# A log-sum-exp scan over rows: 512-row tiles, 32 KiB descriptors, results over the inputs, and the running total by an fp32 broadcast matmul

## The chip, the cores and the metric

The kernel runs on one core of one Trainium2 chip. In the profile of the kernel before, PE multiplies matrices (1,945 matmul records), with the sums in the memory called PSUM; ACT (ScalarE, 385 instructions) and DVE (VectorE, 128) work element by element; SP (SyncE) issues the 128 loads and ACT the 128 stores; 16 DMA engines move the data, in packets. A packet is one record of the trace; here each contiguous run of 16 KiB is one (32,768 records). A packet of 4 bytes is called a semaphore packet: the trace has 16 of them for each load and each store (4,096 in all). The metric is the device time of one execution in microseconds (us). A version is compared with the kernel before it by runs of both on the same chip in the same rounds. A ratio is the mean time of one kernel's runs over the mean of the other's runs of the same rounds, so it is not quite the ratio of the medians that are quoted.

## The reference

```python
B, S, D = 8, 4096, 2048            # x is float32
out[:, 0, :] = x[:, 0, :]
for t in range(1, S):              # out[t] = log(exp(out[t-1]) + exp(x[t]))
    mx = np.maximum(out[:, t-1, :], x[:, t, :])
    out[:, t, :] = mx + np.log(np.exp(out[:, t-1, :] - mx) + np.exp(x[:, t, :] - mx))
```

This is log(cumsum(exp(x))) along the rows of each batch. 268.44 MB are read and 268.44 MB written, by any kernel.

## The kernel before

A tile is 256 rows of one batch: partition p holds rows 2p and 2p+1, which lie next to each other in memory, so each partition's run is 16 KiB. ACT takes exp of the tile into bf16. PE sums over the partitions with triangular matrices: `Li` (inclusive) for the first row, `Ls` (exclusive) for the second, into a PSUM tile of 2,048 columns. The first row's result is the log of PSUM; the second row adds its own exp on VectorE (DVE) first. The complementary triangles `Ui` and `Us` then complete the PSUM tile to the running total, which stays in PSUM for the next tile. Two batches alternate.

```python
xt = xpool.tile([P, 2 * D], f32);  nc.sync.dma_start(out=xt, in_=x_v[b, k])      # 4 buffers
et = epool.tile([P, 2 * D], bf16); nc.scalar.activation(et, xt, ACT.Exp)
for c in range(NC):                                     # 4 chunks of 512 columns
    nc.tensor.matmul(ps[:, lo:hi], Li, et[:, lo:hi], ...)
    nc.tensor.matmul(ps[:, lo:hi], Ls, et[:, D+lo:D+hi], ...)
ot = opool.tile([P, 2 * D], f32)                                                 # 4 buffers
nc.scalar.activation(ot[:, :D], ps, ACT.Ln)
nc.vector.tensor_add(ot[:, D:], ps, et[:, D:])
nc.scalar.activation(ot[:, D:], ot[:, D:], ACT.Ln)
nc.scalar.dma_start(out=o_v[b, k], in_=ot)
# ... then, for all but the last tile, matmuls with Ui and Us into the same ps
```

The softmax here doesn't subtract the row's maximum and nothing guards it: scores larger than these inputs give would overflow.

Of the kernel before, what the change touches and what calls it, by code (L numbers as in the profile page):

```python
# [1 line left out]

# [4 lines left out]


@with_exitstack
def kernel(  # L10
    ctx: ExitStack,
    tc: tile.TileContext,
    x: bass.AP,
    out: bass.AP,
):
    nc = tc.nc
    nc.scalar.preload_act_table_set("natural_log_exp_and_others")  # L17
    f32 = mybir.dt.float32
    bf16 = mybir.dt.bfloat16
    ACT = mybir.ActivationFunctionType  # L20

    B, S, D = x.shape
    P = 128
    SB = 256
    NBLK = S // SB
    FD = 512
    NC = D // FD
    PAIR = 2

    const = ctx.enter_context(tc.tile_pool(name="const", bufs=1))  # L30
    Li = const.tile([P, P], bf16)
    masks.make_upper_triangular(nc, Li, val=1.0, diag=True)
    Ls = const.tile([P, P], bf16)
    masks.make_upper_triangular(nc, Ls, val=1.0, diag=False)
    Ui = const.tile([P, P], bf16)
    masks.make_lower_triangular(nc, Ui, val=1.0, diag=False)
    Us = const.tile([P, P], bf16)
    masks.make_lower_triangular(nc, Us, val=1.0, diag=True)

    xpool = ctx.enter_context(tc.tile_pool(name="xpool", bufs=4))  # L40
    epool = ctx.enter_context(tc.tile_pool(name="epool", bufs=4))
    opool = ctx.enter_context(tc.tile_pool(name="opool", bufs=4))
    ppool = ctx.enter_context(tc.tile_pool(name="ppool", bufs=1, space=bass.MemoryType.PSUM))

    x_v = x.rearrange("b (k p two) d -> b k p (two d)", p=P, two=2)
    o_v = out.rearrange("b (k p two) d -> b k p (two d)", p=P, two=2)

    for bp in range(0, B, PAIR):
        psums = [
            ppool.tile([P, D], f32, name=f"ps_{bp}_{j}", tag=f"ps{j}")  # L50
            for j in range(PAIR)
        ]
        for k in range(NBLK):
            for j in range(PAIR):
                b = bp + j
                ps = psums[j]

                xt = xpool.tile([P, 2 * D], f32)
                nc.sync.dma_start(out=xt, in_=x_v[b, k])  # L59

                et = epool.tile([P, 2 * D], bf16)
                nc.scalar.activation(et, xt, ACT.Exp)  # L62

                for c in range(NC):
                    lo, hi = c * FD, (c + 1) * FD
                    nc.tensor.matmul(  # L66
                        ps[:, lo:hi], Li, et[:, lo:hi],
                        start=(k == 0), stop=False, skip_group_check=True,
                    )
                    nc.tensor.matmul(  # L70
                        ps[:, lo:hi], Ls, et[:, D + lo : D + hi],
                        start=False, stop=False, skip_group_check=True,
                    )

                ot = opool.tile([P, 2 * D], f32)
                nc.scalar.activation(ot[:, :D], ps, ACT.Ln)  # L76
                nc.vector.tensor_add(ot[:, D:], ps, et[:, D:])  # L77
                nc.scalar.activation(ot[:, D:], ot[:, D:], ACT.Ln)  # L78

                nc.scalar.dma_start(out=o_v[b, k], in_=ot)  # L80

                if k < NBLK - 1:
                    for c in range(NC):
                        lo, hi = c * FD, (c + 1) * FD
                        nc.tensor.matmul(  # L85
                            ps[:, lo:hi], Ui, et[:, lo:hi],
                            start=False, stop=False, skip_group_check=True,
                        )
                        nc.tensor.matmul(  # L89
                            ps[:, lo:hi], Us, et[:, D + lo : D + hi],  # L90
                            start=False, stop=False, skip_group_check=True,
                        )


# [1 line left out]
_INS = ['x']  # L96
_OUTS = [((8, 4096, 2048), 'float32')]


# [23 lines left out]
```

## Time and profile before

| | before |
|---|---|
| time, median of 3 | 1259.54 us (1259.22 to 1260.03) |
| span of the profiled execution | 1257.6 us |
| 16 KiB data packets | 32,768 |
| rate in the middle of the run | 430.5 GB/s (packet records, 120 to 1100 us) |

These are lines of the page of the kernel before: the span, the engines' busy time, the busy share of the DMA engines and their rate in 40 slices of the span, the packets, the DMA queues (q1 carries the loads, q10 the stores, q8 and q14 are named "instruction" by the trace), and the chain of waits by engine and by line.

```profile
span 1257.6 us, 5168 instructions
...
PE 645.3 (51%) x1945; PEld 239.4 (19%) x1984; DVE 293.0 (23%) x128; ACT 915.9 (73%) x385; POOL 1.9 (0%) x12
...
DMA  9999999999999999999999999999999999999997
GB/s 390 429 431 432 431 430 430 431 431 430 431 430 433 430 430 432 430 431 430 431 431 431 429 433 430 430 431 430 433 429 431 430 429 433 431 431 430 433 430 326
DMA packets 36888, 537.21 MB, mean 427 GB/s; under 512 B 4096, under 2 KB 4096, under 8 KB 4096
...
q1 hardware_dynamic: 18432, 268.44, 50.0%
q10 hardware_dynamic: 18432, 268.44, 49.9%
q8 instruction: 15, 0.25, 0.1%
q14 instruction: 9, 0.07, 0.0%
...
DMA 71%; ACT 26%; PE 1%; issue 1%; DVE 0%; ACTq 0%; SPq 0%
```

The DMA row is full in every slice but the last, and no compute engine is above 73%.

These are groups of the same page: line, engine, operation, shapes, count, then busy time and the mean of one in ns, then the idle time before them and what ended it.

```profile
L77 DVE TENSOR_TENSOR ot<-ps,et 128x2048 f32<-128x2048 f32 x128 | 293.0, 2291 | 949.4 <-ACT ot L76 949.4
L76 ACT ACTIVATE ot<-ps 128x2048 f32<-128x2048 f32 x128 | 239.8, 1873 | 319.2 <-DMA out_dram<-ot 284.9
L62 ACT ACTIVATE et<-xt 128x4096 bf16<-128x4096 f32 x128 | 461.7, 3607 | 7.9 <-DMA xt<-in_x_dram 7.9
```

ACT waits 285 us for stores to free an output buffer and only 8 us for loads: a DMA-bound kernel whose stores hold everything up.

These are stages of the same execution (from and to in us, length, busy time of each engine with counts, PE clock, share of the 16 DMA engines in use, GB/s): one in the middle and three at the end.

```profile
120.00:600.00 480.00, 255.20 (x753) 93.90 (x768) 112.29 (x49) 347.59 (x147) 0.00 (x0) 0.73 1.01 431
...
1232.00:1238.00 6.00, 5.41 (x20) 1.92 (x17) 0.05 (x1) 5.92 (x3) 0.00 (x0) 0.80 1.02 434
1238.00:1244.00 6.00, 0.09 (x1) 0.00 (x0) 4.43 (x2) 5.19 (x3) 0.00 (x0) 0.76 0.54 229
1244.00:1251.00 7.00, 0.00 (x0) 0.00 (x0) 0.00 (x0) 0.51 (x1) 0.00 (x0) 0.50 0.98 414
```

The DMA share falls to 0.54 from 1238 to 1244 us, while ACT and DVE finish the last two tiles.

### The profile page before, as it was taken

The numbers are of one execution on the slowest core, as the hardware profiler recorded it, in microseconds if no ns is written. First come the engines' busy times: TensorE is split into PE (matmuls) and PEld (weight loads), VectorE is DVE, ScalarE is ACT, GpSimd is POOL, SyncE is SP. The second block draws the span as 40 slices with busy tenths as digits, with TensorE's granted clock in tenths as the row PEclk, the third lists the DMA queues.
The fourth block names the chain that finished last, engine by engine and source line by source line (L and its number), as shares of the span: only waits on it lengthen the run. The fifth ranks groups of instructions, "written<-read, shape, count | busy, mean of one in ns | idle before, by whom it ended". The sixth has DMA issues, their size and how long they took to land.

```text
span 1257.6 us, 5168 instructions
## 1 busy us (share of the span) xinstructions
PE 645.3 (51%) x1945; PEld 239.4 (19%) x1984; DVE 293.0 (23%) x128; ACT 915.9 (73%) x385; POOL 1.9 (0%) x12
## 2 busy tenths in 40 slices
PE   3554554554545555455354555455544454555542
PEld 1221211121112222122111221112211121112210
DVE  1222222222222222222222222222222222222222
ACT  7976667777777777766777777777776666777775
POOL 0000000000000000000000000000000000000000
PEclk9877767776777687776668677786778878677686
DMA  9999999999999999999999999999999999999997
GB/s 390 429 431 432 431 430 430 431 431 430 431 430 433 430 430 432 430 431 430 431 431 431 429 433 430 430 431 430 433 429 431 430 429 433 431 431 430 433 430 326
DMA packets 36888, 537.21 MB, mean 427 GB/s; under 512 B 4096, under 2 KB 4096, under 8 KB 4096
## 3 DMA queue, kind: packets, MB, share of 16 engines
q1 hardware_dynamic: 18432, 268.44, 50.0%
q10 hardware_dynamic: 18432, 268.44, 49.9%
q8 instruction: 15, 0.25, 0.1%
q14 instruction: 9, 0.07, 0.0%
HBM read 268.44 MB, written 268.44 MB: 427 GB/s over the span
## 4 chain that ended last, share of the span: by engine, by line
DMA 71%; ACT 26%; PE 1%; issue 1%; DVE 0%; ACTq 0%; SPq 0%
DMA out_dram<-ot 70%; ACT et L62 13%; ACT ot L76 7%; ACT ot L78 7%; DMA xt<-in_x_dram 1%; DVE ot L77 0%; PE ps L66 0%; PE ps L70 0%; PE ps L85 0%; PE ps L89 0%; ACTq L76 0%; ACTq L80 0%; SPq L59 0%
## 5 line engine op out<-in xcount | busy, mean ns | idle before, releaser
L85 PE MATMUL ps<-et,Ui 128*128 128x512 bf16 x480 | 265.4, 553 | 511.6 <-DVE ot L77 509.2
L77 DVE TENSOR_TENSOR ot<-ps,et 128x2048 f32<-128x2048 f32 x128 | 293.0, 2291 | 949.4 <-ACT ot L76 949.4
L76 ACT ACTIVATE ot<-ps 128x2048 f32<-128x2048 f32 x128 | 239.8, 1873 | 319.2 <-DMA out_dram<-ot 284.9
L62 ACT ACTIVATE et<-xt 128x4096 bf16<-128x4096 f32 x128 | 461.7, 3607 | 7.9 <-DMA xt<-in_x_dram 7.9
L66 PE MATMUL ps<-et,Li 128*128 128x512 bf16 x512 | 228.0, 445 | 81.2 <-ACT et L62 79.6
L89 PE MATMUL ps<-et,Us 128*128 128x512 bf16 x463 | 261.9, 566 | 0.0
L78 ACT ACTIVATE ot<-ot 128x2048 f32<-128x2048 f32 x128 | 238.9, 1899 | 0.7 <-DVE ot L77 0.7
L70 PE MATMUL ps<-et,Ls 128*128 128x512 bf16 x490 | 211.0, 431 | 0.0
L89 PEld LDWEIGHTS <-Us 128*128 128x128 bf16 x480 | 61.1, 127 | 630.0 <-issue 618.7
L70 PEld LDWEIGHTS <-Ls 128*128 128x128 bf16 x512 | 57.7, 113 | 170.8 <-issue 137.0
L85 PEld LDWEIGHTS <-Ui 128*128 128x128 bf16 x480 | 61.0, 127 | 99.1 <-issue 74.5
L66 PEld LDWEIGHTS <-Li 128*128 128x128 bf16 x512 | 59.7, 117 | 98.1 <-issue 59.6
L17 ACT ACT_TABLE_LOAD x1 | 1.3, 1283 | 0.8 <-PEq L107 0.8
masks.py:102 POOL TENSOR_SCALAR_AFFINE_SELECT Us<-Us 128x128 bf16<-128x128 bf16 x1 | 0.3, 293 | 0.0
masks.py:66 POOL TENSOR_SCALAR_AFFINE_SELECT Li<-Li 128x128 bf16<-128x128 bf16 x1 | 0.3, 292 | 0.0
masks.py:66 POOL TENSOR_SCALAR_AFFINE_SELECT Ls<-Ls 128x128 bf16<-128x128 bf16 x1 | 0.3, 292 | 0.0
masks.py:102 POOL TENSOR_SCALAR_AFFINE_SELECT Ui<-Ui 128x128 bf16<-128x128 bf16 x1 | 0.3, 292 | 0.0
masks.py:65 POOL MEMSET Li<- 128x128 bf16 x1 | 0.2, 204 | 0.3 <-POOLq L107 0.3
masks.py:65 POOL MEMSET Ls<- 128x128 bf16 x1 | 0.2, 204 | 0.0
masks.py:101 POOL MEMSET Ui<- 128x128 bf16 x1 | 0.2, 204 | 0.0
masks.py:101 POOL MEMSET Us<- 128x128 bf16 x1 | 0.2, 204 | 0.0
L107 POOL MEMSET const-bfloat16-1.0<- 128x1 bf16 x1 | 0.1, 101 | 0.0
(3 smaller groups left out, 0.3 us busy)
## 6 DMA issues: line engine op xcount, KB each, us to landing
xt<-in_x_dram SPq DMA_DIRECT2D x128, 2048.0 KB, 28.7
out_dram<-ot ACTq DMA_DIRECT2D x128, 2048.0 KB, 30.0
```

What stands on the lines that cost most here:

```text
L17: nc.scalar.preload_act_table_set("natural_log_exp_and_others")
L62: nc.scalar.activation(et, xt, ACT.Exp)
L66: nc.tensor.matmul(ps[:, lo:hi], Li, et[:, lo:hi], start=(k == 0), stop=False, skip_group_check=True,)
L70: nc.tensor.matmul(ps[:, lo:hi], Ls, et[:, D + lo : D + hi], start=False, stop=False, skip_group_check=True,)
L76: nc.scalar.activation(ot[:, :D], ps, ACT.Ln)
L77: nc.vector.tensor_add(ot[:, D:], ps, et[:, D:])
L78: nc.scalar.activation(ot[:, D:], ot[:, D:], ACT.Ln)
L85: nc.tensor.matmul(ps[:, lo:hi], Ui, et[:, lo:hi], start=False, stop=False, skip_group_check=True,)
L89: nc.tensor.matmul(ps[:, lo:hi], Us, et[:, D + lo : D + hi], start=False, stop=False, skip_group_check=True,)
L107: nc = _bacc.Bacc("TRN2", target_bir_lowering=False, num_devices=1)
```

## The change

The intent is fewer and larger DMA packets, and a shorter tail. A tile becomes 512 rows (4 rows a partition, 32 KiB runs); the results overwrite the inputs in one pool of five 4 MB tiles; the work inside a tile goes in pieces of 512 columns; the last tile is also loaded and stored in those pieces, in 2 KiB descriptors. DVE copies the first row's sums out of PSUM and adds the other rows one after another. The total of a piece is the last partition's last row, spread to all partitions of the next tile's PSUM bank by an fp32 matmul with a matrix that is 1 in its last row; `Ui` and `Us` go. The core of the diff:

```diff
-    SB = 256
+    R = 4
+    LAG = 2
-    xpool = ctx.enter_context(tc.tile_pool(name="xpool", bufs=4))
-    opool = ctx.enter_context(tc.tile_pool(name="opool", bufs=4))
+    iopool = ctx.enter_context(tc.tile_pool(name="iopool", bufs=5))
+    spool = ctx.enter_context(tc.tile_pool(name="spool", bufs=3))
+    def load(b, k):
+        t = iopool.tile([P, R, D], f32, name=f"io_{b}_{k}", tag="io")
+        if (b, k) == tiles[-1]:
+            for c in range(NC):
+                nc.sync.dma_start(out=t[:, :, cols(c)], in_=x_v[b, k][:, :, cols(c)])
+        else:
+            nc.sync.dma_start(out=t, in_=x_v[b, k])
+    def front(b, k, c):                       # load at c == 0
+        nc.scalar.activation(et, t[:, :, cols(c)], ACT.Exp)
+        for r in range(R):
+            nc.tensor.matmul(ps, Li if r == 0 else Ls, et[:, r, :], ...)
+        nc.vector.tensor_copy(st[:, 0, :], ps)
+        for r in range(1, R):
+            nc.vector.tensor_add(st[:, r, :], st[:, r - 1, :], et[:, r, :])
+    def carry(b, k, c):
+        nc.tensor.matmul(bank(b, k + 1, c), last, sums[b, k, c][:, R - 1, :], start=True, ...)
+    def back(b, k, c):
+        nc.scalar.activation(t[:, :, cols(c)], sums.pop((b, k, c)), ACT.Ln)
+        if (b, k) == tiles[-1]:
+            nc.scalar.dma_start(out=o_v[b, k][:, :, cols(c)], in_=t[:, :, cols(c)])
+        elif c == NC - 1:
+            nc.scalar.dma_start(out=o_v[b, k], in_=t)
+    for n, piece in enumerate(pieces):
+        front(*piece)
+        if n >= 1:
+            carry(*pieces[n - 1])
+        if n >= LAG:
+            back(*pieces[n - LAG])
```

(`...` in it marks arguments that were cut; the removed loop is the one shown in the section before last.)

More of the change, by code (lines that the diff above doesn't have):

```diff
@@ L16 @@
     nc = tc.nc
-    nc.scalar.preload_act_table_set("natural_log_exp_and_others")
     f32 = mybir.dt.float32
@@ L20 @@
     ACT = mybir.ActivationFunctionType
+    nc.scalar.preload_act_table_set("natural_log_exp_and_others")
     B, S, D = x.shape
     P = 128
-    SB = 256
-    NBLK = S // SB
+    R = 4
+    NBLK = S // (P * R)
     FD = 512
     NC = D // FD
-    PAIR = 2
+    LAG = 2
     const = ctx.enter_context(tc.tile_pool(name="const", bufs=1))
@@ L34 @@
     masks.make_upper_triangular(nc, Ls, val=1.0, diag=False)
-    Ui = const.tile([P, P], bf16)
-    masks.make_lower_triangular(nc, Ui, val=1.0, diag=False)
-    Us = const.tile([P, P], bf16)
-    masks.make_lower_triangular(nc, Us, val=1.0, diag=True)
-    xpool = ctx.enter_context(tc.tile_pool(name="xpool", bufs=4))
-    epool = ctx.enter_context(tc.tile_pool(name="epool", bufs=4))
-    opool = ctx.enter_context(tc.tile_pool(name="opool", bufs=4))
-    ppool = ctx.enter_context(tc.tile_pool(name="ppool", bufs=1, space=bass.MemoryType.PSUM))
@@ L45 @@
-    x_v = x.rearrange("b (k p two) d -> b k p (two d)", p=P, two=2)
-    o_v = out.rearrange("b (k p two) d -> b k p (two d)", p=P, two=2)
-    for bp in range(0, B, PAIR):
-        psums = [
-            ppool.tile([P, D], f32, name=f"ps_{bp}_{j}", tag=f"ps{j}")
-            for j in range(PAIR)
-        ]
-        for k in range(NBLK):
-            for j in range(PAIR):
-                b = bp + j
-                ps = psums[j]
-                xt = xpool.tile([P, 2 * D], f32)
-                nc.sync.dma_start(out=xt, in_=x_v[b, k])
-                et = epool.tile([P, 2 * D], bf16)
-                nc.scalar.activation(et, xt, ACT.Exp)
-                for c in range(NC):
-                    lo, hi = c * FD, (c + 1) * FD
-                    nc.tensor.matmul(
-                        ps[:, lo:hi], Li, et[:, lo:hi],
-                        start=(k == 0), stop=False, skip_group_check=True,
-                    )
-                    nc.tensor.matmul(
-                        ps[:, lo:hi], Ls, et[:, D + lo : D + hi],
-                        start=False, stop=False, skip_group_check=True,
-                    )
-                ot = opool.tile([P, 2 * D], f32)
-                nc.scalar.activation(ot[:, :D], ps, ACT.Ln)
-                nc.vector.tensor_add(ot[:, D:], ps, et[:, D:])
-                nc.scalar.activation(ot[:, D:], ot[:, D:], ACT.Ln)
-                nc.scalar.dma_start(out=o_v[b, k], in_=ot)
-                if k < NBLK - 1:
-                    for c in range(NC):
-                        lo, hi = c * FD, (c + 1) * FD
-                        nc.tensor.matmul(
-                            ps[:, lo:hi], Ui, et[:, lo:hi],
-                            start=False, stop=False, skip_group_check=True,
-                        )
-                        nc.tensor.matmul(
-                            ps[:, lo:hi], Us, et[:, D + lo : D + hi],
-                            start=False, stop=False, skip_group_check=True,
-                        )
@@ new lines @@
+    last = const.tile([P, P], f32)
+    nc.gpsimd.memset(last, 1.0)
+    nc.gpsimd.affine_select(
+        out=last, in_=last, compare_op=mybir.AluOpType.is_ge, fill=0.0,
+        base=-(P - 1), pattern=[[0, P]], channel_multiplier=1,
+    )
+    iopool = ctx.enter_context(tc.tile_pool(name="iopool", bufs=5))
+    epool = ctx.enter_context(tc.tile_pool(name="epool", bufs=4))
+    spool = ctx.enter_context(tc.tile_pool(name="spool", bufs=3))
+    ppool = ctx.enter_context(tc.tile_pool(name="ppool", bufs=2, space=bass.MemoryType.PSUM))
@@ new lines, with cols @@
+    x_v = x.rearrange("b (k p r) d -> b k p r d", p=P, r=R)
+    o_v = out.rearrange("b (k p r) d -> b k p r d", p=P, r=R)
+    tiles = [(b, k) for b in range(B) for k in range(NBLK)]
+    pieces = [(b, k, c) for b, k in tiles for c in range(NC)]
+    io = {}
+    sums = {}
+    banks = {}
+    def cols(c):
+        return slice(c * FD, (c + 1) * FD)
+    def load(b, k):
+        t = iopool.tile([P, R, D], f32, name=f"io_{b}_{k}", tag="io")
+        io[b, k] = t
+        if (b, k) == tiles[-1]:
[3 more added lines that the diff above has]
+            nc.sync.dma_start(out=t, in_=x_v[b, k])
@@ new lines, in bank @@
+    def bank(b, k, c):
+        if (b, k, c) not in banks:
+            banks[b, k, c] = ppool.tile([P, FD], f32, name=f"ps_{b}_{k}_{c}", tag=f"ps{c}")
+        return banks[b, k, c]
+    def front(b, k, c):
+        if c == 0:
+            load(b, k)
+        t = io[b, k]
+        et = epool.tile([P, R, FD], bf16, name="et")
+        nc.scalar.activation(et, t[:, :, cols(c)], ACT.Exp)
+        ps = bank(b, k, c)
+        for r in range(R):
+            nc.tensor.matmul(
+                ps, Li if r == 0 else Ls, et[:, r, :],
+                start=(k == 0 and r == 0), stop=(r == R - 1), skip_group_check=True,
+            )
+        st = spool.tile([P, R, FD], f32, name="st")
+        nc.vector.tensor_copy(st[:, 0, :], ps)
+        for r in range(1, R):
+            nc.vector.tensor_add(st[:, r, :], st[:, r - 1, :], et[:, r, :])
+        sums[b, k, c] = st
@@ new lines, in carry @@
+    def carry(b, k, c):
+        if k < NBLK - 1:
+            nc.tensor.matmul(
+                bank(b, k + 1, c), last, sums[b, k, c][:, R - 1, :],
+                start=True, stop=False, skip_group_check=True,
+            )
+    def back(b, k, c):
+        t = io[b, k]
+        nc.scalar.activation(t[:, :, cols(c)], sums.pop((b, k, c)), ACT.Ln)
[3 more added lines that the diff above has]
+            nc.scalar.dma_start(out=o_v[b, k], in_=t)
@@ L96 @@
+    for n, piece in enumerate(pieces):
[4 more added lines that the diff above has]
+            back(*pieces[n - LAG])
+    for piece in pieces[-LAG:]:
+        back(*piece)
 _INS = ['x']
```

## The prediction

> **What bounds the kernel now.** The DMA engines: on the page DMA is 9 tenths in every slice but the last, and 429 to 433 GB/s move in nearly all; the stage table gives DMA share 1.01 at 431 GB/s from 60 to 1230 us. ACT is busy 73%, PE 51%, DVE 23%. In the chain of waits 70% is the store of results. 268.44 MB are read and as many written; the change leaves that so.
>
> In the packet records a 16 KiB packet takes 611 ns, an 8 KiB one (instruction load) 309 ns at best, a semaphore packet 9 ns. A line through the two sizes (estimate): 302 ns per 8 KiB plus 7 ns a packet. [...]
>
> **Terms on the critical path, per DMA engine:**
> - 2,048 packets of 16 KiB become 1,008 of 32 KiB plus the last tile's; 7 ns each: about -7 us.
> - Semaphore packets: 256 to about 134, at 9 ns: -1 us.
> - The last tile goes in 512-column chunks of 2 KiB descriptors: 256 packets at an estimated 82 ns against 16 of 1,215 ns: +1.7 us.
> - End: before, the packet records show the engines emptying between the last two stores (down to 1 of 16 in use), about 2.8 us lost, as ACT still works on the last pair of tiles. After, stores of two earlier 4 MB tiles (about 20 us) still queue while the last pieces are computed: -2.5 us.
> - Start: first packet 1.8 us into the span, as before; five loads (about 48 us) are queued until stores begin: 0.
>
> **Off the path:**
> - ACT: 512 exps and logs of 128x2048 at about 1.9 us (from 3,607 ns for 4,096 columns, 1,899 for 2,048): 970 us, 78%; per tile 15 us against 19.5 us of DMA.
> - DVE: 2,048 columns take 2.29 us, so 512 about 0.7 us; four a piece, 256 pieces: 710 us, 57%.
> - PE: per piece four bf16 matmuls of 430 to 560 ns and the carry. [...] The carry is needed four pieces later and the bank is doubled, so its latency hides.
> - The log of a tile's last two pieces now stands on ACT behind the next tile's exp, so the store waits for the next load; five buffers (97 us of period) cover a lifetime of about 20 load + 20 wait + 8 + 20 store.
>
> **Prediction.** Span 1257.6 - 7 - 1 + 1.7 - 2.5 = 1248.5; the time lies 1.9 us above the span: 1250 us, 0.8% faster, 8 in 10 between 1244 and 1258. Faster by over 2%: 1%. Within 2%: 94%. Slower by over 2%: 5%.
>
> **What would show it.** About 22,400 packets instead of 36,888, a 32 KiB packet at about 1,215 ns; 432 to 434 GB/s in the middle slices; a last slice well above 326 GB/s; DMA 9 tenths throughout; ACT waiting for loads, not for stores; PE waits not on the chain.
>
> **What would make it wrong.** 32 KiB descriptors are split (then about 1257), or the wider pitch slows HBM; [...] the store held behind the next load starves the load queue, showing as DMA gaps once a tile; 2 KiB packets cost far more than 82 ns.

1257.6 - 7 - 1 + 1.7 - 2.5 is 1248.8, where the prediction has 1248.5; with the 1.9 us on top that is 1250.7, where it has 1250. The 0.7 us for 512 columns on DVE is the estimate; a quarter of the 2.29 us would be 0.57.

## The result

| | before | after |
|---|---|---|
| time, median of 4 | 1259.38 us | 1259.70 us (1259.63 to 1259.88) |
| ratio to before | 1 | 1.0002 (0.9985 to 1.0019) |
| span | 1257.6 us | 1257.9 us |
| rate, 120 to 1100 us | 430.5 GB/s | 432.4 GB/s |
| a large data packet | 611 ns for 16 KiB | 1,213 ns for 32 KiB |

The change is worth nothing, where 9 us were forecast and 1244 us to 1258 us was the range. Lines of the page of the kernel after, as of before:

```profile
span 1257.9 us, 5492 instructions
...
PE 638.5 (51%) x1472; PEld 215.0 (17%) x1472; DVE 703.3 (56%) x1024; ACT 930.0 (74%) x513; POOL 1.5 (0%) x10
...
DMA  9999999999999999999999999999999999999997
GB/s 400 433 429 431 432 432 433 432 432 433 433 434 433 429 433 433 432 433 432 432 433 432 433 432 433 432 433 433 434 433 432 434 433 431 433 433 433 433 381 299
DMA packets 22399, 537.22 MB, mean 427 GB/s; under 512 B 2144, under 2 KB 2144, under 8 KB 6240
...
q1 hardware_dynamic: 11184, 268.44, 49.7%
q10 hardware_dynamic: 11184, 268.44, 49.6%
q8 instruction: 11, 0.18, 0.1%
q14 instruction: 20, 0.16, 0.0%
...
DMA 69%; ACT 14%; DVE 5%; PE 5%; issue 5%; SPq 1%; ACTq 0%; DVEq 0%
```

The packets did become 32 KiB (16,128 of them), the packet count of 22,399 is the predicted one, and the middle slices rose from about 431 to 433. What was won there was lost in the last two slices: 381 and 299 instead of 430 and 326. And q14 fetches 20 packets of instructions instead of 9, while DVE has 1,024 instructions instead of 128 (below, with 768 of them, q14 has 16).

The groups that answer to those of before:

```profile
L98 DVE TENSOR_TENSOR st<-st,et 128x512 f32<-128x512 f32 x768 | 530.9, 692 | 43.4
L110 ACT ACTIVATE io<-st 128x2048 f32<-128x2048 f32 x256 | 484.6, 1894 | 15.0 <-DMA io<-in_x_dram 10.7
L88 ACT ACTIVATE et<-io 128x2048 bf16<-128x2048 f32 x256 | 485.3, 1897 | 301.1 <-DMA io<-in_x_dram 301.1
L103 PE MATMUL ps<-st,last 128*128 128x512 f32 x448 | 304.6, 769 | 137.8 <-DVE st L98 136.6
```

ACT now waits for loads (311.8 us) and not for stores, as forecast, and the durations on ACT (1,897 and 1,894 ns) and DVE (692 ns) are near their estimates. The carry appears as two matmul records of 769 ns (448 records for 224 carries), 1.5 us in all.

The stages at the end of the kernel after:

```profile
120.00:600.00 480.00, 244.89 (x563) 83.43 (x564) 268.35 (x391) 354.64 (x197) 0.00 (x0) 0.77 1.00 432
...
1220.00:1226.00 6.00, 0.00 (x0) 0.00 (x0) 0.37 (x1) 0.00 (x0) 0.00 (x0) 0.57 0.58 216
1226.00:1232.00 6.00, 2.71 (x6) 1.21 (x6) 0.69 (x1) 4.67 (x3) 0.00 (x0) 0.50 0.48 171
1232.00:1238.00 6.00, 3.67 (x10) 0.93 (x8) 5.12 (x8) 6.00 (x4) 0.00 (x0) 0.78 0.52 220
```

For 18 us the DMA engines are half idle. ACT's own timeline there (start, length, what; in brackets the wait before it):

```profile
1214.67 1.90 ACT L110 ACTIVATE io<-st 128x2048 f32<-128x2048 f32 x1
1227.33 1.91 ACT L88 ACTIVATE et<-io 128x2048 bf16<-128x2048 f32 x1 [10.77 <-DMA io<-in_x_dram]
...
1234.67 0.34 ACTq L114 DMA_DIRECT2D out_dram<-io  x1
```

ACT waits 10.8 us for the first chunk of the last tile, and the store of the tile before it, which stands behind that on ACT, is issued only at 1234.7 us, when the store queue has been empty for about 9 us even on the DMA engine that is last.

The packet records (start, queue, size and duration of each packet; they do not name the DMA engine) show why that chunk was late. From 1199 to 1208 us both queues had work:

```
after, 1199 to 1208 us     mean engines in use    GB/s
load of the last tile       1.09 of 16            27     (2 KiB packets of 84 ns)
stores                     14.97 of 16            403    (32 KiB packets of 1,213 ns)
```

In these 9 us 112 load packets and 112 store packets began. If an engine takes one packet from each queue in turn, the load's share of time is 84 / (84 + 1213) = 6.5%, or 1.04 of 16 engines. The trace agrees with such turns, of one 2 KiB or one 32 KiB record. So in this stretch the small packets got little beside the large ones.

### The profile page after: what moved, and what is told of

It is laid out like the page before. It is cut to its first block, busy times and chain, and to the rows that moved or that the text cites. A ratio compares the mean times of both kernels' runs of the same rounds, so it can differ in the third digit from the quotient of the medians.

```text
span 1257.9 us, 5492 instructions
## 1 busy us (share of the span) xinstructions
PE 638.5 (51%) x1472; PEld 215.0 (17%) x1472; DVE 703.3 (56%) x1024; ACT 930.0 (74%) x513; POOL 1.5 (0%) x10
## 2 busy tenths in 40 slices
DMA packets 22399, 537.22 MB, mean 427 GB/s; under 512 B 2144, under 2 KB 2144, under 8 KB 6240
## 4 chain that ended last, share of the span: by engine, by line
DMA 69%; ACT 14%; DVE 5%; PE 5%; issue 5%; SPq 1%; ACTq 0%; DVEq 0%
DMA io<-in_x_dram 67%; ACT io L110 8%; ACT et L88 5%; DVE st L98 4%; PE ps L91 3%; DMA out_dram<-io 2%; PE ps L103 2%; DVE st L96 1%; SPq L74 1%; ACTq L114 0%; ACTq L110 0%; DVEq L98 0%; ACTq L88 0%; DVEq L96 0%; SPq L76 0%
## 5 line engine op out<-in xcount | busy, mean ns | idle before, releaser
L88 ACT ACTIVATE et<-io 128x2048 bf16<-128x2048 f32 x256 | 485.3, 1897 | 301.1 <-DMA io<-in_x_dram 301.1
L98 DVE TENSOR_TENSOR st<-st,et 128x512 f32<-128x512 f32 x768 | 530.9, 692 | 43.4
L110 ACT ACTIVATE io<-st 128x2048 f32<-128x2048 f32 x256 | 484.6, 1894 | 15.0 <-DMA io<-in_x_dram 10.7
L96 DVE COPY st<-ps 128x512 f32<-128x512 f32 x256 | 176.7, 690 | 498.3 <-PE ps L91 492.9
L103 PE MATMUL ps<-st,last 128*128 128x512 f32 x448 | 304.6, 769 | 137.8 <-DVE st L98 136.6
L91 PE MATMUL ps<-et,Li 128*128 128x512 bf16 x256 | 124.9, 488 | 465.7 <-ACT et L88 463.9
L91 PE MATMUL ps<-et,Ls 128*128 128x512 bf16 x768 | 287.8, 497 | 0.0
L91 PEld LDWEIGHTS <-Ls 128*128 128x128 bf16 x768 | 89.4, 116 | 697.7 <-issue 668.1
L103 PEld LDWEIGHTS ps<-st,last 128*128 128x128 f32 x448 | 94.7, 234 | 250.8 <-DVE st L98 228.3
L91 PEld LDWEIGHTS <-Li 128*128 128x128 bf16 x256 | 30.8, 120 | 77.6 <-issue 70.2
```

Of the source, the lines that this page charges most:

```text
L88: nc.scalar.activation(et, t[:, :, cols(c)], ACT.Exp)
L91: nc.tensor.matmul(ps, Li if r == 0 else Ls, et[:, r, :], start=(k == 0 and r == 0), stop=(r == R - 1), skip_group_check=True,)
L96: nc.vector.tensor_copy(st[:, 0, :], ps)
L98: nc.vector.tensor_add(st[:, r, :], st[:, r - 1, :], et[:, r, :])
L103: nc.tensor.matmul(bank(b, k + 1, c), last, sums[b, k, c][:, R - 1, :], start=True, stop=False, skip_group_check=True,)
L110: nc.scalar.activation(t[:, :, cols(c)], sums.pop((b, k, c)), ACT.Ln)
```

## The experiments

Fourteen versions ran, all with the right result, each beside the kernel before in the same rounds (four to six timed runs of a version). Theory A at the start: the last load is starved by turn-taking, so the stores run dry, and that costs the 9 us. Its rivals are named in the expectations.

### The last tile's load whole; load and store whole

```diff
-        if (b, k) == tiles[-1]:
-            for c in range(NC):
-                nc.sync.dma_start(out=t[:, :, cols(c)], in_=x_v[b, k][:, :, cols(c)])
-        else:
-            nc.sync.dma_start(out=t, in_=x_v[b, k])
+        nc.sync.dma_start(out=t, in_=x_v[b, k])
```

> The last tile's load as one transfer of 32 KiB packets; its store stays in 2 KiB chunks. Theory A (the DMA engines take packets in turn from the load and the store queue, so 2 KiB load packets beside 32 KiB store packets get about 1 engine of 16, the last load lands 10 to 15 us late, and the stores behind it run dry): the last load gets about half of the engines, lands before 1217 us instead of 1235, the DMA gap of 1220 to 1236 us goes, 1249 to 1253 us. Rival B (the gap comes because the store of the last tile but one stands on ACT behind the last tile's exp, whatever the packets): at most 3 us less than 1259.7. Rival C (steady rate is not really better): 1257 or more.

Measured: 1257.16 us, ratio 0.9981 (0.9968 to 0.9995). From 1199 to 1208 us the last load now had 8.7 of 16 engines, and it landed at 1221 us instead of 1235. With packets of one size the load got about half, as turns of one packet would give, so the turn-taking holds in both runs. But the time fell by 2.5 us only, not 7 to 11: Theory A's account of the time falls. The time alone fits Rival B, and Rival C too; B is tested by the change of order below, C by the version with 16 KiB packets.

The second version stores the last tile whole, too (the condition on `tiles[-1]` in `back` goes as well).

> The last tile's load and its store as single transfers of 32 KiB packets. Theory A: as e1, the 2 KiB penalty of the store (about 1.4 us by the packets' 88 ns against 75.8) goes too, but the last store begins only when all four pieces are done, at a moment when the store before it has just ended: 1248 to 1252 us, within 2 us of e1. If the store's chunking was worth its cost, e3 is slower than e1 by over 2 us.

Measured: 1256.44 us, ratio 0.9976 (0.9963 to 0.9988). It lies above the expected 1248 to 1252 us, but within 2 us of the version before. It is 3.3 us less than after, and the 2 KiB packets' own time accounts for most of that: their mean was 90.6 ns (loads) and 87.7 ns (stores), so 256 of them took 22.8 us an engine, against 19.4 us for 16 packets of 1,213 ns. Packets on one engine overlap by 3.5 ns (see below), and 240 overlaps more take 0.8 us off this difference, which leaves 2.6 us. Chunking the last store was not worth its cost. This version, with no small packets, is the base of most of what follows.

### Stores of the four tiles before it in 2 KiB packets, too

```diff
+        elif c == NC - 1 and (b, k) in tiles[-5:]:
+            for j in range(NC):
+                nc.scalar.dma_start(out=o_v[b, k][:, :, cols(j)], in_=t[:, :, cols(j)])
```

> The change as it is, load of the last tile in 2 KiB packets, but the stores of the four tiles before it also in 2 KiB packets. Theory A: load and store packets are then equal in size, so the last load gets about half of the engines instead of 1 of 16 while stores run, lands before 1222 us, the gap mostly goes; against that 4 stores cost about 1.5 us more each: 1255 to 1260 us. Rival D (2 KiB loads are slow of themselves, or by their issue): the load still gets 1 to 3 engines while stores run and lands after 1227 us, time 1263 us or more.

Measured: 1269.64 us, ratio 1.0081. The point of it held: beside stores of equal packets the 2 KiB load had 11.9 of 16 engines from 1190 to 1202 us (the stores did not fill their half) and landed at 1217 us. So these 2 KiB loads are not slow of themselves. The time missed (it lies where Rival D had it, but D's late landing did not come), by a side effect not foreseen: the issue of such stores held ACT, 15.7 us for the four chunks of one tile, and ACT stood idle for 27.7 us before its next exp.

### ACT finishes the last tile but one first

```diff
+        if n == len(pieces) - NC:          # before the first piece of the last tile
+            carry(*pieces[n - 1])
+            while done < n:                # the two pieces still open
+                back(*pieces[done]); done += 1
```

> The change as it is, but ACT finishes the last tile but one (its last two logs and its store) before the first exp of the last tile. Rival B: the store is there when the queue runs dry, the gap goes, 1251 to 1254 us. Theory A: the store of the last tile but one is issued about 15 us earlier and fills the gap of 1220 to 1235 us, but the 2 KiB load is then starved by that store too and lands later than 1235 us, and the last tile is computed with nothing left to move: 1255 to 1260 us.

Measured: 1258.96 us with 2 KiB loads kept (1257.96 to 1262.1), ratio 1.0000. The last load landed at 1240 us, later than the 1235 us of the kernel after, as Theory A said; the rival's 1251 to 1254 us is out. The same order with the last load whole:

> Last load whole, store in 512-column chunks, and ACT finishes the last tile but one (its logs and its store) before the last tile: the gap of about 5 us between the last stores closes on the 14 engines that are ahead. Rival F: 1251 to 1253 us. Theory E: the engine that ends last was never idle, so no more than 1.5 us less than 1257.2: 1255.5 to 1257.5 us.

Measured: 1257.33 us, ratio 0.9984. This decides what the gap is worth. These are its stages (first fence) and those of the version with load and store whole (second fence):

```profile
1226.00:1232.00 6.00, 3.67 (x8) 1.11 (x8) 5.07 (x8) 6.00 (x4) 0.00 (x0) 0.50 1.02 437
1232.00:1238.00 6.00, 1.87 (x4) 0.41 (x3) 5.65 (x9) 4.51 (x3) 0.00 (x0) 0.50 0.92 378
1238.00:1244.00 6.00, 0.00 (x0) 0.00 (x0) 0.00 (x0) 1.78 (x1) 0.00 (x0) 0.50 0.86 326
1244.00:1251.00 7.00, 0.00 (x0) 0.00 (x0) 0.00 (x0) 0.13 (x1) 0.00 (x0) 0.50 0.69 259
```

```profile
1226.00:1232.00 6.00, 3.37 (x9) 0.89 (x8) 5.00 (x8) 6.00 (x5) 0.00 (x0) 0.78 0.66 284
1232.00:1238.00 6.00, 1.44 (x3) 0.41 (x3) 4.46 (x7) 5.45 (x4) 0.00 (x0) 0.50 1.02 437
1238.00:1244.00 6.00, 0.00 (x0) 0.00 (x0) 0.78 (x2) 1.91 (x1) 0.00 (x0) 0.50 0.48 202
1244.00:1251.00 7.00, 0.00 (x0) 0.00 (x0) 0.00 (x0) 0.00 (x0) 0.00 (x0) 0.50 1.05 451
```

(Columns as in the stages above; the one before the last is the share of the DMA engines.) With the new order the DMA share from 1226 to 1232 us is 1.02 instead of 0.66, and 13 of the 16 engines end 2 to 3 us sooner: by the packet records the median engine ends the last store at 1248.5 us instead of 1251.5. The time is not shorter, since one engine still ends at 1254.6 us (1253.3 in the second fence, where no store is cut into 2 KiB packets). The exact pair to the new order is the first version above, with the same transfers in the old order: its median engine ended at 1250.6 us, its last at 1254.2, and the times are 1257.16 (old) and 1257.33 us (new). So the idle time of the others is off the critical path, and Theory A and Rival B are done with. What matters is the one engine.

### Theory E: the engine that ends last also fetches VectorE's instructions

The packet records of the version with load and store whole can be followed backwards on the engine that ends last, since a packet starts 3.5 ns before the one ahead of it ends. The records do not name the engine, so this chain is inferred; where two engines are in step it is ambiguous:

```
the last engine, from the start to its end at 1253.3 us
first packet                                               1.8 us
1,024 packets of 32 KiB at 1,213 - 3.5 ns               1,238.5 us    (1/16 of all bytes)
12 packets of 8 KiB of q14, about 0.9 us each             10.7 us    (at 55, 155, 258, 358, 468, 568,
                                                                      671, 780, 883, 983, 1093, 1193 us)
semaphore packets, two long packets at the start        about 2 us
gaps                                                         none
```

An instruction packet takes 309 ns itself, and the load packet after it lasts about 590 ns longer than 1,213. Twelve in this time, one about every 100 us, fits DVE's 1,024 instructions. The other engines have none of these packets; the median engine stands idle for about 7 us near the end (1224.5 to 1229.3 and 1239.2 to 1241.7 us) and ends at 1251.5 us. The lag of the last engine behind the median engine, at the landing of a load, grows by about 0.9 us at each of the fetches, to 9.3 us at the last load. The second engine, 6.2 us behind at the last load, has seven such packets of another stream (six before that load), which fits ACT's 513 instructions; they cost it about 0.6 us each. The packet behind a fetch tells the streams apart: load packets behind the twelve are 531 to 633 ns late, those behind ACT's 245 to 315 ns. The 16 KiB packets of q8, which fit PE's instructions (see the carry issued twice), are not in the chain of the last engine, and they do not pile up on one engine: in the kernel after, at the 27th load, after four of them, five engines were 1.1 to 1.6 us behind the median engine, one 2.7 and the last, after five fetches, 4.4 us.

The others wait for this engine: each load ends with 16 semaphore packets, and ACT's first exp starts after the last of them (0.35 us or more, in 63 tiles of the kernel after). The median engine had its part of the last load at 1211.3 us, the last engine at 1220.6, and ACT's exp began at 1221.1. The kernel after itself has the same twelve fetches (58 to 1201 us). Its last engine, followed in the same way, works without a gap from the last fetch through its stores (to 1226.0 us) and its share of the last load (to 1234.9), stands idle for 0.6 us and starts the held store at 1235.5, as the other 15 do; all 16 end within 0.4 us (1256.3 to 1256.6). So the 18 us of half idle engines were, for the most part, a wait of the others for this one.

The trace shows the fetches in two instruction queues, q8 and q14; q14 carries what fits DVE and what fits ACT. The waits of the kernel after list none of DVE for an instruction, so there no cost shows; the DMA engine that carries the fetch pays about 0.9 us each time, and in this DMA-bound kernel that shows.

Theory E says: the number of DVE instructions sets the time, by 0.9 us for each fetch. Its rival F says: these fetches are a coincidence, and instructions are free.

### Four small DVE writes more a piece

```diff
+    tiny = const.tile([P, 4], f32)
...
+        for r in range(R):
+            nc.vector.memset(tiny[:, r:r+1], 0.0)
```

> The whole-transfer version (1256.4 us) plus four tiny writes of one column on VectorE in each of the 256 pieces: 1,024 more VectorE instructions, no more data. Theory E (one DMA engine also fetches an engine's instructions in 8 KiB packets, is never idle, ends last and sets the time; the other engines have 8 us to spare): about 8 more fetches at 0.9 us each on that engine, so 1262 to 1265 us, and 8 KiB instruction packets rise from 20 to about 28. Rival F (the time is set by the gap between the last stores on all engines): VectorE has room (56% busy), so within 1 us of 1256.4.

Measured: 1281.99 us (1275.18 to 1286.6), ratio 1.0173; q14 28 packets instead of 20. Neither E's number (eight fetches, the author's estimate, were to cost 7 us) nor F's came out, and the run tests neither. The edit did not do what was meant: in the trace all the small writes, on which no other instruction depends, run at the start, from 0.9 to 87.0 us (duration in ns, then first and last start in us):

```profile
L97 DVE MEMSET tiny<- x1024: 59/59/59, 0.9 to 87.0; 128x1 f32 x171
```

And the packet records show a second cost: 836 load packets were more than 60 ns late (57 in the base), in sum 342 us over the 16 engines, while stores kept their time, and the rate of the middle of the run fell to 424.6 GB/s. Of these, 767 start after 500 us, long after the last small write. The new tile also moved every other tile by 16 bytes, so two controls follow. The first moves every tile by the same 16 bytes and writes the small tile once only:

> The whole-transfer version with one more 16-byte tile allocated ahead of the 4 MB tiles and written once, so that these start 16 bytes later in SBUF; no other instruction added. If the slow load packets of the run with the tiny writes (836 of them over 60 ns late) came from the address: steady rate near 425 GB/s and 1272 us or more. If they came from the 1,024 VectorE writes: 432.4 GB/s and 1256 to 1257 us.

Measured: 1256.46 us, ratio 0.9976, as without it. The address is not the cause. The second adds the four instructions without a new tile, by copying single columns of PSUM that are copied anyway:

```diff
+        for r in range(R):
+            nc.vector.tensor_copy(st[:, 0, r:r+1], ps[:, r:r+1])
```

> The whole-transfer version (1256.4 us) plus four one-column copies on VectorE in each piece, into columns that the sums overwrite anyway or write again with the same value: 1,024 more VectorE instructions as in the run with the tiny writes, but no new tile, so the tiles stay at their addresses. Theory E: about 8 more instruction packets of 8 KiB, 0.9 us each on the DMA engine that ends last: 1262 to 1265 us, steady rate unchanged at 432.4 GB/s. If the 1282 us of the tiny writes came from the VectorE instructions themselves: 1275 us or more. Rival F: within 1 us of 1256.4.

Measured: 1267.08 us (1265.53 to 1271.15), ratio 1.0066, above the expected 1262 to 1265 us. Here the copies are spread over the run (about 120 in each 100 us), and the fetches of DVE rose from 12 to 20 as meant. Up to 600 us Theory E comes out: the rate is the base's (432.3 GB/s from 120 to 600 us), 9 load packets are late from 100 to 600 us against 8, and at the load that lands at 620 us the last engine lags by 9.3 us after ten fetches, where it lags by 4.0 us after six in the base. So F, for which these fetches cost nothing, is out. Later load packets come late here as well (281 in the whole run), and stores too (248 against 13), which leaves 429.3 GB/s in the middle, though the copies go on as before. In both runs the late packets set in only after the last engine was over 9 us behind. So it is not shown that DVE's writes slow the loads, and why packets then come late stays open. Adding is a poor test of E. The clean test takes instructions away.

### The same transfers with 256 DVE instructions fewer

```diff
-        nc.vector.tensor_copy(st[:, 0, :], ps)
-        for r in range(1, R):
+        nc.vector.tensor_add(st[:, 1, :], ps, et[:, 1, :])
+        for r in range(2, R):
...
-        nc.scalar.activation(t[:, :, cols(c)], sums.pop((b, k, c)), ACT.Ln)
+        nc.scalar.activation(t[:, 0, cols(c)], banks[b, k, c], ACT.Ln)
+        nc.scalar.activation(t[:, 1:, cols(c)], sums.pop((b, k, c))[:, 1:, :], ACT.Ln)
```

(Load and store whole, as in the base.) The copy of the first row out of PSUM goes; ACT takes that row's log from PSUM, which splits its log in two.

> The whole-transfer version (1256.4 us) without VectorE's copy of the first row out of PSUM: VectorE has 768 instead of 1,024 instructions, ACT takes the log of the first row from PSUM by itself (769 instead of 513 instructions, about 90 us more busy). Transfers unchanged. Theory E: 9 or 10 instead of 12 instruction packets on the DMA engine that ends last, 0.9 us each: 1253 to 1255 us, and the last load lands 6.5 to 7.5 us after the median engine instead of 9.3. If the lag of that engine has another cause: 1256 to 1257 us, or more, as ACT has more to do.

Measured: 1253.32 us (1253.27 to 1253.77), ratio 0.9951 (0.9937 to 0.9965). The busy times and instruction queues of the base (first fence) and of this version (second):

```profile
PE 633.8 (51%) x1443; PEld 215.2 (17%) x1472; DVE 703.1 (56%) x1024; ACT 930.0 (74%) x513; POOL 1.5 (0%) x10
...
q14 instruction: 20, 0.16, 0.0%
```

```profile
PE 702.2 (56%) x1472; PEld 221.8 (18%) x1472; DVE 529.4 (42%) x768; ACT 944.4 (75%) x769; POOL 1.5 (0%) x10
...
q14 instruction: 16, 0.13, 0.0%
```

By the packets behind them, DVE's fetches are 8 instead of 12, and ACT's 7 as before within the span. The last engine's lag at the last load is 6.0 us instead of 9.3, and the time is 3.1 us less, near the 4 x 0.9 us of Theory E. The transfers and their order are the same, and PE and ACT are busier than in the base, so they can't have given the time. Nor did the late load packets of the last two runs: 69 were more than 60 ns late, against 57 in the base. ACT's 256 instructions more cost nothing that shows: its fetches are, by the same marks, on the second engine, 5.0 us behind.

### Pieces of 1,024 columns

A second way to fewer DVE instructions (512), with the sums written into the input tile, the last load whole, the last tile but one finished first, and the last store in two halves:

```diff
-    FD = 512
+    FD = 1024
...
-        st = spool.tile([P, R, FD], f32, name="st")
+        st = t[:, :, cols(c)]
```

> Last load whole, ACT finishes the last tile but one before the last tile, and pieces of 1,024 columns with the sums held in the tile itself: half as many VectorE and ACT instructions, the last stores in two pieces of 4 KiB packets. Theory E: 6 instead of 12 fetches on the slowest DMA engine, 5 us less than the same at 512 columns: 1249 to 1252 us. Rival F: no better than the 512-column version beside it (within 1.5 us), or worse, as larger pieces lengthen the tail.

Measured: 1257.51 us (1255.95 to 1259.42), ratio 0.9984. The step of E held: the last engine's lag at the last load fell to 3.9 us, and all engines now end together at 1252.6 us. The expected time did not: with larger pieces the last tile takes longer to compute, ACT waited 6.7 and 5.3 us there, and now the last engine stands idle too, for about 1 us before 1242 us. How much of the miss this makes is not shown. The next version keeps 512 columns in the last tile alone and does not finish the tile before it first:

> Meant to beat both: pieces of 1,024 columns with the sums in the tile, the last tile in pieces of 512 columns, its load whole, its store in two halves of 4 KiB packets, no early finish of the tile before it. Theory E: half of the VectorE and ACT instructions, so the last DMA engine has 5 us less to fetch, and the tail no longer waits 7 us for the last tile's large pieces: 1250 to 1253 us. Otherwise 1255 us or more.

Measured: 1253.31 us, ratio 0.9950 (0.9938 to 0.9963), just outside the expected 1250 to 1253 us. Both together, pieces of 1,024 columns and no copy (390 DVE instructions):

> The 1,024-column version with small last pieces (1253.3 us), and VectorE's copy of the first row left out as in the last run: about 390 VectorE instructions instead of 1,024. If the instruction packets still set the time: 1250.5 to 1252.5 us. If the gap on the other engines between the last stores now sets it: 1252.5 to 1254 us.

Measured: 1252.94 us (1252.74 to 1257.06), ratio 0.9959 (0.9946 to 0.9973). The remedies don't add up, and what bounds the combined version was not tested. In its trace one engine still ends at 1249.8 us, 2.0 us after the median; in that of the version before it all end within 0.7 us. The three best versions are within each other's intervals, 0.4 to 0.5% faster than the kernel before.

### What 32 KiB packets are worth alone

Each load and store of the base is split into two, which gives 16 KiB packets and 36,896 of them, as before the change:

```diff
-            nc.sync.dma_start(out=t, in_=x_v[b, k])
+        for h in (slice(0, 2), slice(2, 4)):
+            nc.sync.dma_start(out=t[:, h, :], in_=x_v[b, k][:, h, :])
```

(The store likewise.)

> The whole-transfer version, but each tile's load and store as two transfers of two rows a partition, so 16 KiB packets as before the change. If the packet size alone raised the steady rate from 430.5 to 432.4 GB/s, the rate falls back to 430.5 and the time rises by about 5.4 us to 1261 to 1263 us. Rival: the rate comes from the different order of loads and stores, then it stays at 432.4 and 1256 to 1257 us.

Measured: 1261.70 us, ratio 1.0017 (1.0003 to 1.0030), 430.46 GB/s in the middle. Three things follow. The rate fell back as expected, so it comes from the packets' size and not from the order of loads and stores, and Rival C is out. Against the base, the large packets are worth 1261.70 - 1256.44 = 5.3 us. And against the kernel before, with about the same packets, the rest of the change costs 0.17%, or about 2.2 us, where the prediction had a gain.

### The fp32 carry issued twice

> The whole-transfer version with every fp32 carry matmul issued twice (same result). If the carry is off the path: 1256 to 1258 us, PE busy up by about 300 us; its instruction packets (16 KiB) rise from 11 to about 15 but go to the DMA engines in turn, not to the last one. If PE or the carry bounds the time: 1270 us or more.

Measured: 1256.33 us, ratio 0.9975, equal to the base. The page of this version:

```profile
PE 788.6 (63%) x1920; PEld 302.7 (24%) x1920; DVE 703.2 (56%) x1024; ACT 930.2 (74%) x513; POOL 1.5 (0%) x10
...
q8 instruction: 15, 0.25, 0.1%
```

PE is busy 155 us more (about 300 were expected) and q8 has four packets more (which engines carried them was not followed in this run), and the time does not move. The carry is off the path, as predicted.

## Why the prediction was wrong

The measured pieces are: 1259.4 - 5.3 (large packets) + 2.2 (the rest of the change, with 16 KiB packets) + 3.3 (the last tile in 2 KiB chunks: after against load and store whole) = 1259.6, where 1259.7 was measured. That the sum comes out proves nothing, since each piece is the difference of two versions along one chain from before to after; it only shows that runs on different chips, each beside the kernel before, agree. What the pieces say is which term was mis-sized.

**What was right.** The kernel is DMA-bound before and after (DMA 9 tenths in all slices but the last, no compute engine above 74%). The packet count, the 32 KiB duration (1,213 ns for 1,215), ACT's 930 us (estimate 970), DVE's 703 us (estimate 710), the wait of ACT for loads, and a hidden carry all came out. The 32 KiB runs were not split (16,128 records of that size), memory did not slow down (432.4 GB/s against 430.5), PE did not limit (the doubled carry cost no time), and there was no gap once a tile (DMA 9 tenths in all slices but the last).

**"-7 us" and "-1 us": mis-sized.** The two terms measured -5.3 together. Packets on one engine overlap by 3.5 ns. Two of 611 ns in place of one of 1,213 ns lose 9 ns, less the one overlap more: 5.5 ns x 1,024 = 5.6 us. The prediction added durations as if packets stood end to end. The gain forecast for semaphore packets does not show beside this.

**"+1.7 us": mis-sized.** It measured +3.3: a 2 KiB packet took 88 to 91 ns and not 82, which with the overlaps makes 2.6 us, and the last engine stood idle for 0.6 us before the held store. That its load would starve beside 32 KiB stores (1.09 of 16 engines) was not foreseen; but loading it whole gained 2.5 us in all, of which about 1.5 us is the packets' own time ((90.6 x 128 - 8 x 1,213) ns, less 120 overlaps of 3.5 ns), so the starvation itself cost about 1 us.

**"End: -2.5 us": the step that failed.** "About 2.8 us lost" was read from the number of engines in use, a mean over 16. The engine that ends last in the kernel before had no idle time there: it ended at 1256.3 us, the others at 1253.0, after 2 to 5 us idle. There was nothing to be won. The other half of the step failed as well: the stores of two earlier tiles did not still queue while the last pieces were computed. The last of them was issued at 1234.7 us, behind ACT's wait for the last load, which the prediction had seen and taken to be covered by five buffers. In place of a gain came a cost: the change gave DVE eight times as many instructions, their fetches all go to one DMA engine (by the chain of packets), and in the version with load and store whole 12 of them cost that engine 10.7 us. "DVE: off the path" counted busy time alone. Removing four fetches gave back 3.1 us, which is the shown part. That all 12 are worth 0.9 us each is read from the packet records, not from a run without any.

**What stays open.** What holds the last engine of the kernel before 3.3 us behind the others: it has few DVE fetches (two by the mark of the late load packet behind them, at 319 and 944 us), and its packets could not be followed backwards without doubt. So the +2.2 us is measured as a whole, but not split into fetches gained and something else lost. Open too is why load packets came late in the two runs with added DVE instructions, and what bounds the combined version.

## What to carry to other kernels

In a DMA-bound kernel, ask which DMA engine ends last and whether it ever stands idle: here a gap in the mean of 16 engines cost nothing while one engine lagged. Count instructions as DMA traffic: VectorE stood idle 44% of the time, and 256 of its instructions fewer still gave 3.1 us, through the fetches. Look in the trace whether an added instruction runs where it was meant to; the small writes here did not. Small packets beside large ones in another queue got a small share here (1.09 of 16 engines), and no run shows a gain from cutting the last tile into 2 KiB packets.
